# Two kinds of elementwise work of the recurrences go from VectorE to GpSimd

## The chip, the cores and the metric

The kernel runs on one core of a Trainium2 chip. The metric is the device time of one execution in microseconds (us), the median of several runs. The engines are named as in the profile: PE is TensorE (PEld its weight loads), DVE is VectorE, ACT is ScalarE, POOL is GpSimd, and SP is the engine from whose queue nearly all loads are issued.

## The reference

Two transformer blocks act on one sequence of 256 tokens with 1024 features, all in float32. The first block (a half feed-forward, a Hyena long convolution and differential attention side by side, another half feed-forward) is not touched by the change. The second block begins with a projection `u = h @ w_in`, whose columns feed several parts:

```python
u_rwkv = centred_token_shift(u[..., :RWKV_COLS], mu_prev, mu_next)
q, k_att, v_att, gl_rwkv, gl_attn = jnp.split(u[..., RWKV_COLS:], ATT_SPLITS, axis=-1)
y_rwkv = rwkv7_bidir(u_rwkv, ...)          # 8 heads of 64, one scan forward, one backward
y_attn = banded_gqa_attention(q, k_att, v_att, sink)
merged = sigmoid(gl_rwkv) * (y_rwkv @ w_proj_rwkv) + sigmoid(gl_attn) * (y_attn @ w_proj_attn)
x = x + merged @ w_out
x = x + expert_choice_moe(rms_norm(x, g), w_router, w_gate, w_up, w_down)   # 16 experts
return rms_norm(x, g_final)
```

One step of the scan, for each head, with a 64x64 state `S`:

```python
s_kk = jnp.einsum('bhij,bhj->bhi', S, kk_t)
S = S * w_t - s_kk[..., None] * (a_t * kk_t) + v_t[..., None] * k_t
y_t = jnp.einsum('bhij,bhj->bhi', S, r_t)
```

The expert part reads 16 x 3 matrices of 1024x1024 float32, some 200 MB, which no other part of the program approaches.

## The kernel before, in words

**Matmuls in three passes.** Where full float32 precision is wanted at a fast rate, a number is split into a high part (a cast by ACT, line 139) and a low part (the number less its high part, a subtraction with two inputs in SBUF, line 140). `mm3` (lines 145 to 147) multiplies high by high, high by low and low by high into one PSUM bank. `weights` (line 125) loads a chunk of weights into `raw` from SP's queue (line 130) and splits it in pieces of 128x512, into `whi` and `wlo`; for all weights DVE makes the low part. In the second block's pool there are two buffers each of `raw`, `whi` and `wlo`: a new load waits until the low part of the chunk two before has been made, and a new cast until PE is through with that chunk.

**The recurrences.** Instead of a scan over tokens, `lane` (line 1280) computes one direction of one pair of heads in four chunks of 64 tokens, with matmuls of 64x64. First it makes the decay products on PE (line 1296) and their exponentials on ACT, `W` and `Wv`; from these it makes four factors of 128x256: `t0`, `t1` (the factors of the rank-one updates and of the keys, lines 1307 to 1312) and the two halves of `kr` (line 1313: decay times normalised key, line 1314: decay times receptance). All on DVE. Matmuls of `kr` with `t0` and `t1` follow (line 1383, called from `mm_heads`), their masking on DVE (line 1323), then the inverse of a triangular matrix: a chain of 14 small DVE operations (lines 1426, 1427) and several products. Then four dependent steps of state and output, each a ping-pong between PE and DVE or ACT. `rwkv_out` normalises and gates the result; its last product, on DVE, is line 1489, after the matmul of the gates in line 1488.

There are eight such recurrences and four attention jobs. `lanes` (line 1225) keeps four of them active in four slots and takes one step of each in turn.

**The filling.** Between their steps it takes steps of the rest of the projection (`fill`): 22 chunks of 1024x128 weights for q, k, v and the gates, each 24 matmuls of 128x256, in two steps of 12. These `gemm_steps` are called with `whole=True`; no other call is. After the recurrences the outputs are split (`yh`, `yl`, line 140), projected with w_proj_rwkv and w_proj_attn, and so on. The loads of w_proj_attn, w_out and of all expert weights go to a ring of 41 buffers of 512 KB, whose memory is that of the recurrences' tiles.

**What sets the order.** The program's framework schedules each engine's queue itself from the order of the calls, the priorities and its own model of costs. A changed engine or cost therefore changes the order on all engines, also of instructions that the diff does not name.

Of the kernel before, what the change touches and what calls it, by code (L numbers as in the profile page):

```python
# [16 lines left out]
ALU = mybir.AluOpType  # L17
# [51 lines left out]
class Net:  # L69
# [52 lines left out]
        self.wp = self.pool(f"wp{n_raw}{n_split}", 1, side="left", es=self.wes)  # L122


    def weights(self, src, ring=False):

        nc = self.nc
        kt, cols = src.shape[1:]
        raw = self.raw_tile() if ring else self.wp.tile([128, kt, cols], F32, name="raw", tag="raw", bufs=self.n_raw)
        nc.sync.dma_start(out=raw, in_=src)  # L130
        hi = self.wp.tile([128, kt, cols], F32R, name="whi", tag="whi", bufs=self.n_split)
        lo = self.wp.tile([128, kt, cols], F32R, name="wlo", tag="wlo", bufs=self.n_split)
        n = max(1, min(kt, CUT // cols))
        for k in range(0, kt, n):
            self.split(raw[:, k:k + n], hi[:, k:k + n], lo[:, k:k + n])
        return hi, lo

    def split(self, src, hi, lo, eng=None):
# [14 lines left out]
    def gemm_steps(self, src, x, n, consume, c0=0, c1=None, steps=1, ring=False, whole=False):  # L153


        i = 0
        for c in range(c0, src.shape[0] if c1 is None else c1):
            hi, lo = self.weights(src[c], ring)
            kt, w = src.shape[2:]
            for m in range(w // 128):  # L160
                ps = self.mm([128, n])
                s = slice(m * 128, m * 128 + 128)
                for k in range(kt):
                    with self.tc.high_priority() if whole and k % (kt // steps) else ExitStack():
                        self.mm3(ps, (hi[:, k, s], lo[:, k, s]), (x[0][:, k, :], x[1][:, k, :]), k == 0, k == kt - 1)
                    if k < kt - 1 and (k + 1) % (kt // steps) == 0:
                        yield
                consume(i, ps)
                i += 1
                yield  # L170
# [290 lines left out]
    def first_ffn(self):  # L461
# [21 lines left out]
        with ExitStack() as es2:  # L483
# [13 lines left out]
            def weights(n):  # L497
# [3 lines left out]
                for i in range(2):  # L501
                    self.split(w[i][0][:, s], w[i][1][:, s], w[i][2][:, s])

            weights(0)
            diag = []
            for i in range(4):
# [16 lines left out]
            for f in range(KT + 1):  # L523
                if f < KT:
                    if f + 1 < KT:
                        raws.append(self.ada_load(f + 1, tmp))
                        if f % 2:
                            weights(f // 2 + 1)
                    row = self.ada_rows_of(raws[f], tmp)
                    ps = self.aux([128, 2 * T])  # L530
                    self.turned(ps, x, f, diag)
                if f:
                    products(f - 1, (0, 1))
                if f < KT:
                    a = self.ada_columns(f, row)
                    for i in range(2):
                        t = self.wk.tile([128, T], F32, name="nt", tag="nt", bufs=3)
                        nc.scalar.activation(out=t, in_=ps[:, cut[i]], func=AF.Identity, scale=a[:, i:i + 1],
                                             bias=self.mods[:, f, i:i + 1])
                        self.split(t, h[0][:, f, cut[i]], h[1][:, f, cut[i]])  # L540
                if f:
                    products(f - 1, (2, 3))
# [737 lines left out]
    def lane(self, L, p, d, ur):  # L1280

        nc = self.nc
# [3 lines left out]
        W, kr, Wv, t0, t1 = (L[x] for x in ("W", "kr", "Wv", "t0", "t1"))  # L1286
# [19 lines left out]
        a, kk = self.ar[:, d, p, :], self.kkn[:, p, :]  # L1306
# [3 lines left out]
        yield  # L1310
        nc.vector.tensor_tensor(out=t0, in0=t0, in1=Wv, op=ALU.mult)
        nc.vector.tensor_tensor(out=t1, in0=t1, in1=Wv, op=ALU.mult)
        nc.vector.tensor_tensor(out=kr[:, 0, :], in0=W[:, 1, :], in1=kk, op=ALU.mult)
        nc.vector.tensor_tensor(out=kr[:, 1, :], in0=W[:, 0, :], in1=ur[:, p, :], op=ALU.mult)
        yield

        for src, strict, incl in ((bb, ab, hb), (kh, ak, hk)):
# [659 lines left out]
```

## Time and profile before

| | |
|---|---|
| median of 3 runs | 1811.67 us (1810.1 to 1814.51) |
| the profiled execution itself | 1813.05 us |
| its span, first to last instruction | 1811.3 us |
| busy PE / DVE / ACT / POOL | 1687.9 / 1009.7 / 706.9 / 19.9 us |
| granted TensorE clock, mean | 0.925 |
| read from HBM | 394.59 MB, 218 GB/s over the span |

The profile is of one execution. Busy times are sums over instructions; matmuls overlap each other, so that a busy PE can still hold short stalls. A granted clock of 1.00 is TensorE's higher level, 2.4 GHz. The recurrences lie between about 1080 and 1275 us; up to there and a little beyond PE is nearly always busy, and from about 1290 us to the end DMA is.

### The profile page before, as it was taken

The page shows a single profiled execution, that of the slowest core. Times are in us where ns is not written, and L with a number is a line of the kernel's source. Part 1 is how long each engine was busy: PE and PEld are TensorE (multiplying, and loading weights), DVE is VectorE, ACT ScalarE, POOL GpSimd, SP SyncE. Part 2 cuts the span into 40 slices and gives each one's busy share as a digit, 9 for nine tenths or more (in the row PEclk, how much of TensorE's full clock was granted, in tenths as well). Part 3 has the DMA queues.
Part 4 walks back from the last instruction along what each step waited for, and adds up shares of the span by engine and source line. Part 5 has one row for each costly group of instructions (what it writes and reads, how often), then busy time and mean ns, then how long its engine had stood idle before and what let it go on. Part 6 is the DMA issues. An engine that isn't in the chain of part 4 may idle for free.

```text
span 1811.3 us, 33886 instructions
## 1 busy us (share of the span) xinstructions
PE 1687.9 (93%) x13847; PEld 1275.4 (70%) x13847; DVE 1009.7 (56%) x2502; ACT 706.9 (39%) x1515; POOL 19.9 (1%) x41
## 2 busy tenths in 40 slices
PE   8999999999999999999999999999999878787776
PEld 5788787788998889999999798888874222222222
DVE  3888776768987776676665768877740000000001
ACT  3532223657545568456444653456640000000001
POOL 0000000000000000000000000000010000000000
PEclk9999999999999999999999899999999676767678
DMA  8666673423432214546543331112799999999997
GB/s 330 217 219 231 220 260 112 133 82 121 155 108 94 91 70 140 187 148 248 187 163 117 115 123 61 49 61 76 298 400 400 409 408 409 409 408 409 408 409 303
DMA packets 97768, 397.85 MB, mean 220 GB/s; under 512 B 11227, under 2 KB 13708, under 8 KB 84044
## 3 DMA queue, kind: packets, MB, share of 16 engines
q1 hardware_dynamic: 91728, 386.97, 56.9%
q10 hardware_dynamic: 3724, 4.77, 0.8%
q0 software_dynamic: 2160, 3.94, 0.8%
q8 instruction: 109, 1.79, 0.4%
q14 instruction: 47, 0.39, 0.1%
HBM read 394.59 MB, written 1.05 MB: 218 GB/s over the span
## 4 chain that ended last, share of the span: by engine, by line
PE 68%; DMA 19%; DVE 8%; ACT 3%; issue 1%; DVEq 0%; ACTq 0%; SPq 0%
PE mm L145 13%; PE mm L147 12%; PE mm L146 12%; DMA raw<-exp_w_down 7%; DMA raw<-exp_w_gate 7%; PE mm L1572 4%; PE a L1383 4%; PE at L145 4%; PE at L146 4%; PE at L147 4%; PE a L1740 3%; DMA araw<-w_adat 2%; DMA raw<-exp_w_up 2%; DVE wlo L140 2%; DVE ajunk L310 2%
## 5 line engine op out<-in xcount | busy, mean ns | idle before, releaser
L139 ACT CAST whi<-raw 128x512 fp32r<-128x512 f32 x542 | 309.4, 618 | 260.6 <-PE mm L146 133.1
L140 DVE TENSOR_TENSOR wlo<-raw,whi 128x512 fp32r<-128x512 f32 x542 | 356.5, 686 | 97.8 <-ACT whi L139 93.5
L145 PE MATMUL mm<-hh,whi 128*128 128x256 f32 (+1 forms) x784 | 245.8, 315 | 0.5 <-DVE kl L140 0.5
L147 PE MATMUL mm<-hh,wlo 128*128 128x256 f32 (+1 forms) x784 | 244.9, 314 | 0.5 <-DVE wlo L140 0.2
L146 PE MATMUL mm<-hl,whi 128*128 128x256 f32 (+1 forms) x784 | 244.0, 312 | 0.0
L1707 DVE TENSOR_SCALAR scat<-iota,col 128x256 f32<-128x256 f32 x16 | 6.5, 412 | 275.0 <-PE a L1740 275.0
L145 PEld LDWEIGHTS mm<-hh,whi 128*128 128x128 f32 x784 | 147.2, 188 | 13.2 <-issue 3.5
L146 PEld LDWEIGHTS mm<-hl,whi 128*128 128x128 f32 x784 | 147.3, 188 | 9.9 <-issue 0.8
L147 PEld LDWEIGHTS mm<-hh,wlo 128*128 128x128 f32 x784 | 146.9, 188 | 10.0 <-DVE wlo L140 1.1
L1572 PE MATMUL mm<-raw,ehid 128*32 128x256 f32 x960 | 100.1, 513 | 40.6 <-DMA raw<-exp_w_down 40.2
L1744 ACT COPY ys<-mm 128x256 f32<-128x256 f32 (+1 forms) x20 | 7.2, 362 | 303.4 <-PE mm L1572 293.2
L310 DVE SCALAR_TENSOR_TENSOR ajunk<-araw,scr 128x512 bf16<-128x512 f32 x160 | 110.2, 689 | 27.6 <-DMA araw<-w_adat 25.5
L1572 PE MATMUL mm<-raw,xg 128*32 128x256 f32 x1024 | 103.1, 489 | 20.4 <-DMA raw<-exp_w_gate 20.4
L145 PE MATMUL at<-hh,whi 128*128 128x512 f32 (+1 forms) x352 | 118.7, 337 | 0.0
L147 PE MATMUL at<-hh,wlo 128*128 128x512 f32 (+1 forms) x352 | 118.4, 336 | 0.0
L146 PE MATMUL at<-hl,whi 128*128 128x512 f32 (+1 forms) x352 | 118.1, 336 | 0.0
L145 PE MATMUL mm<-whi,hidh 128*128 128x512 f32 x264 | 105.5, 400 | 1.1 <-ACT hidh L139 0.6
L147 PE MATMUL mm<-whi,hidl 128*128 128x512 f32 x264 | 104.8, 398 | 0.5 <-DVE hidl L140 0.4
L146 PE MATMUL mm<-wlo,hidh 128*128 128x512 f32 x264 | 104.8, 397 | 0.0
L1572 PEld LDWEIGHTS mm<-raw,ehid 128*32 128x32 f32 x960 | 23.7, 123 | 113.7 <-DMA raw<-exp_w_down 95.5
L1572 PE MATMUL a<-raw,xg 128*32 128x256 f32 x1024 | 83.9, 482 | 8.8 <-DMA raw<-exp_w_up 8.8
L145 PE MATMUL mm<-h2h,whi 128*128 128x256 f32 x296 | 89.7, 304 | 0.0
(630 smaller groups left out, 3391.9 us busy)
## 6 DMA issues: line engine op xcount, KB each, us to landing
raw<-exp_w_gate SPq DMA_DIRECT2D x128, 512.0 KB, 10.2
raw<-exp_w_up SPq DMA_DIRECT2D x128, 512.0 KB, 10.2
raw<-exp_w_down SPq DMA_DIRECT2D x120, 512.0 KB, 10.2
raw<-w_ff_in SPq DMA_DIRECT2D x42, 1024.0 KB, 4.8
raw<-w_in SPq DMA_DIRECT2D x32, 1024.0 KB, 4.7
araw<-w_adat SPq DMA_DIRECT2D x56, 512.0 KB, 4.7
raw<-w_ff_out SPq DMA_DIRECT2D x20, 1024.0 KB, 4.9
raw<-w_fill SPq DMA_DIRECT2D x22, 512.0 KB, 3.5
```

Of the source, the lines that this page charges most:

```text
L139: self.high = self.nc.scalar.copy(out=hi, in_=src)
L140: self.low = (eng or self.nc.vector).tensor_tensor(out=lo, in0=src, in1=hi.bitcast(F32), op=ALU.subtract)
L145: nc.tensor.matmul(out=ps, lhsT=w[0], rhs=x[0], start=first, stop=False)
L146: nc.tensor.matmul(out=ps, lhsT=w[0], rhs=x[1], start=False, stop=False)
L147: nc.tensor.matmul(out=ps, lhsT=w[1], rhs=x[0], start=False, stop=last)
L310: nc.vector.scalar_tensor_tensor(out=junk, in0=raw[:, s], scalar=1.0, in1=self.scr[v][:, s], op0=ALU.mult, op1=ALU.mult, accum_out=part[:, ...
L1383: self.nc.tensor.matmul(out=ps[r], lhsT=w[r], rhs=x[r], start=start, stop=stop)
L1572: nc.tensor.matmul(out=ps[q], lhsT=x(k), rhs=raw[:, j, :], start=(k == 0), stop=(k == KT - 1))
L1707: nc.vector.tensor_scalar(out=sc, in0=self.iota[:, 0:T], scalar1=col[:, 0, e:e + 1], scalar2=col[:, 1, e:e + 1], op0=ALU.is_equal, op1=ALU ...
L1740: nc.tensor.matmul(out=acc(tt, j), lhsT=sc[q, tt * 128:tt * 128 + 128], rhs=ys[q], start=False, stop=False)
L1744: nc.scalar.copy(out=ys, in_=ps)
```

## The change

Two edits. In `gemm_steps`, where `whole` is set, that is for the 22 chunks of the filling alone, the low parts of the weights are made by POOL instead of DVE. In `lane`, the two products that make `kr` are made by POOL.

```diff
-    def weights(self, src, ring=False):
+    def weights(self, src, ring=False, low=None):
...
-            self.split(raw[:, k:k + n], hi[:, k:k + n], lo[:, k:k + n])
+            self.split(raw[:, k:k + n], hi[:, k:k + n], lo[:, k:k + n], low)
...
-            hi, lo = self.weights(src[c], ring)
+            hi, lo = self.weights(src[c], ring, self.nc.gpsimd if whole else None)
...
-        nc.vector.tensor_tensor(out=kr[:, 0, :], in0=W[:, 1, :], in1=kk, op=ALU.mult)
-        nc.vector.tensor_tensor(out=kr[:, 1, :], in0=W[:, 0, :], in1=ur[:, p, :], op=ALU.mult)
+        nc.gpsimd.tensor_tensor(out=kr[:, 0, :], in0=W[:, 1, :], in1=kk, op=ALU.mult)
+        nc.gpsimd.tensor_tensor(out=kr[:, 1, :], in0=W[:, 0, :], in1=ur[:, p, :], op=ALU.mult)
```

`split` is not changed; its fourth argument is the engine of the low part, DVE if there is none.

The queues then look as follows. POOL at the start of the recurrences, before: a load, and copies for the inverse (`ip`), one set for each slot.

```order
L821 DMA rope<-rope 128x1024
L1403 COPY ip_10947<-r_10201 128x4x32
L1403 COPY ip_10965<-r_10201 128x4x32
L1403 COPY ip_10983<-r_10201 128x4x32
L1403 COPY ip_11001<-r_10201 128x4x32
```

POOL at the same place now (`wlo` are low parts of the filling, three numbers of `krs` three slots):

```order
L1403 COPY ip_10983<-r_10201 128x4x32
L1403 COPY ip_11001<-r_10201 128x4x32
L140 TENSOR_TENSOR wlo<-raw,whi 128x512
L1313 TENSOR_TENSOR krs_10949<-Ws_10948,kkn 128x256
L1314 TENSOR_TENSOR krs_10949<-Ws_10948,ur 128x256
L1313 TENSOR_TENSOR krs_10967<-Ws_10966,kkn 128x256
L1314 TENSOR_TENSOR krs_10967<-Ws_10966,ur 128x256
L1313 TENSOR_TENSOR krs_10985<-Ws_10984,kkn 128x256
L1314 TENSOR_TENSOR krs_10985<-Ws_10984,ur 128x256
L140 TENSOR_TENSOR wlo<-raw,whi 128x512 x4
```

Four low parts, of the first two chunks, stand before the products of the first three slots, and the next chunks' behind them. The queue goes on with low parts, products of the later recurrences and copies until the last low part, and then come the four loads of lines 1070 and 1073 that before stood right behind the last copy.

PE at the first use of the products, before (`mm<-h2` are fills, of which the last three of a step of 12 are shown):

```order
L145 MATMUL mm<-h2h_10176,whi 128x256
L146 MATMUL mm<-h2l_10184,whi 128x256
L147 MATMUL mm<-h2h_10176,wlo 128x256
L1383 MATMUL a_11033<-krs_10949,t0s_10951 64x128 x8
L1383 MATMUL a_11045<-krs_10949,t1s_10952 64x128 x8
L1383 MATMUL a_11134<-krs_10967,t0s_10969 64x128
L1388 MATMUL a_11056<-ident,t0s_10951 64x64 x6
```

PE at the same place now:

```order
L145 MATMUL mm<-h2h_10180,whi 128x256
L146 MATMUL mm<-h2l_10188,whi 128x256
L147 MATMUL mm<-h2h_10180,wlo 128x256
L1296 MATMUL a_11211<-rc,sg 128x2x128 x2
L1383 MATMUL a_11033<-krs_10949,t0s_10951 64x128 x8
L1383 MATMUL a_11045<-krs_10949,t1s_10952 64x128 x8
L1383 MATMUL a_11134<-krs_10967,t0s_10969 64x128 x2
L1388 MATMUL a_11056<-ident,t0s_10951 64x64 x6
```

A step of 12 fills that stood between the third decay product (line 1296) and the first use of `kr` now stands behind it. Over the whole stage the fills come later: 96 of the 528 stand behind the last recurrence's last matmul, where there were 58, and between the first decay product and the last fill there are 43 separate groups of fills instead of 50.

DVE at the end of the stage, before (`yh`, `yl` are low parts of the outputs, `wlo` here those of w_proj_rwkv):

```order
L1485 TENSOR_TENSOR t1s_11006<-ur,a_13913 128x256
L140 TENSOR_TENSOR yl_14084<-q_10197,yl_14080 128x256
L1486 TENSOR_TENSOR t0s_11005<-t0s_11005,t1s_11006 128x256
L140 TENSOR_TENSOR yl_14085<-q_10197,yl_14081 128x256
L1489 TENSOR_TENSOR ur<-t0s_11005,a_13918 128x256
L140 TENSOR_TENSOR wlo<-raw,whi 128x512 x4
L140 TENSOR_TENSOR yh_14077<-ur,yh_14073 128x256
L1087 TENSOR_TENSOR gates<-mm,gates 128x256 x2
```

DVE at the same place now:

```order
L1489 TENSOR_TENSOR ur<-t0s_11005,a_13918 128x256
L140 TENSOR_TENSOR wlo<-raw,whi 128x512
L140 TENSOR_TENSOR yl_14082<-q_10197,yl_14078 128x256
L140 TENSOR_TENSOR yh_14074<-ur,yh_14070 128x256
L140 TENSOR_TENSOR yh_14075<-ur,yh_14071 128x256
L140 TENSOR_TENSOR yh_14076<-ur,yh_14072 128x256
L140 TENSOR_TENSOR yh_14077<-ur,yh_14073 128x256
L140 TENSOR_TENSOR yl_14083<-q_10197,yl_14079 128x256
L140 TENSOR_TENSOR yl_14084<-q_10197,yl_14080 128x256
L140 TENSOR_TENSOR yl_14085<-q_10197,yl_14081 128x256
L140 TENSOR_TENSOR wlo<-raw,whi 128x512 x3
```

The last recurrence's output (line 1489) now stands before all splits and before three of the four low parts of w_proj_rwkv. On PE the gates' matmul (line 1488), which line 1489 reads, stands before the last 24 fills, where it stood behind the last fill and four projection matmuls. On SP's queue one load of w_proj_attn now stands between the second and the third load of w_proj_rwkv; all four stood behind the fourth.

## Rows read from the trace of the kernel before

**Rows 1.** Page, chain of waits; table of stretches: engine busy (x instructions), clock, DMA.

```profile
PE 68%; DMA 19%; DVE 8%; ACT 3%; issue 1%; DVEq 0%; ACTq 0%; SPq 0%
...
1090.00:1120.00 30.00, 29.42 (x600) 26.24 (x597) 25.09 (x106) 11.45 (x31) 0.30 (x1) 1.00 0.23 73
...
1240.00:1270.00 30.00, 30.00 (x290) 24.05 (x286) 22.18 (x66) 20.59 (x49) 0.00 (x0) 1.00 0.22 71
```

**Rows 2.** Waits of PE's weight loads, 1080 to 1275: us, times, longest; first and last.

```profile
PEld a L1383 <- issue: 2.6, 9, 0.4
...
PEld a L1472 <- PE mm L146: 0.2, 1, 0.2
```

**Rows 3.** DVE's groups, 1080 to 1290: busy us, mean ns, idle before.

```profile
L140 DVE TENSOR_TENSOR wlo<-raw,whi 128x512 fp32r<-128x512 f32 x51 | 34.1, 686 | 9.5 <-ACT whi L139 9.3
...
L1314 DVE TENSOR_TENSOR krs<-Ws,ur 128x256 f32<-128x256 f32 x8 | 3.4, 420 | 0.0
```

**Rows 4.** Timeline of PE near the end of the filling: start, length, instruction.

```profile
1272.52 0.28 PE L146 MATMUL mm<-h2l,whi 128*128 128x256 f32 x1
1272.64 0.28 PE L147 MATMUL mm<-h2h,wlo 128*128 128x256 f32 x1
1272.90 0.68 PE L1472 MATMUL a<-ident,yall 64*64 64x64 f32 x16
1273.51 0.39 PE L145 MATMUL mm<-h2h,whi 128*128 128x256 f32 x1
1273.73 0.28 PE L146 MATMUL mm<-h2l,whi 128*128 128x256 f32 x1
```

**Rows 5.** Timeline of ACT, DVE and PE at the first recurrence's start.

```profile
1079.57 0.60 ACT L1298 ACTIVATE Ws<-a 128x512 f32<-128x512 f32 x1
...
1081.61 0.42 DVE L1313 TENSOR_TENSOR krs<-Ws,kkn 128x256 f32<-128x256 f32 x1
...
1082.68 0.42 DVE L1314 TENSOR_TENSOR krs<-Ws,ur 128x256 f32<-128x256 f32 x1
...
1083.66 1.09 PE L1383 MATMUL a<-krs,t0s 64*64 64x128 f32 x16
```

**Rows 6.** Timeline of POOL and DVE in the routing stage.

```profile
1336.86 6.00 POOL L140 TENSOR_TENSOR hm<-hf,hm 128x256 fp32r<-128x256 f32 x8 [4.34 <-ACT hm L139]
...
1338.48 0.42 DVE L1641 MAX8 top<-at 16x8 f32<-16x256 f32 x1
...
1340.35 0.55 DVE L1647 TENSOR_TENSOR sel<-top,slotmask 16x128 f32<-16x128 f32 x1
...
1344.29 0.26 DVE L1647 TENSOR_TENSOR sel<-top,slotmask 16x128 f32<-16x128 f32 x1
```

**Rows 7.** Timeline of PE, DVE and SP's queue after the filling.

```profile
1274.93 0.28 PE L147 MATMUL mm<-h2h,wlo 128*128 128x256 f32 x1
...
1277.64 2.49 DVE L140 TENSOR_TENSOR wlo<-raw,whi 128x512 fp32r<-128x512 f32 x4
...
1278.38 0.38 PE L147 MATMUL mm<-yh,wlo 128*128 128x256 f32 x1 [1.24 <-DVE wlo L140]
...
1280.05 0.42 DVE L140 TENSOR_TENSOR yh<-ur,yh 128x256 fp32r<-128x256 f32 x1
...
1280.58 2.00 SPq L130 DMA_DIRECT2D raw<-w_proj_attn  x4
...
1281.74 0.28 DVE L1098 TENSOR_TENSOR wr<-wr,pv 128x128 f32<-128x128 f32 x1
```

**Rows 8.** Table of stretches, the first in which loads run without pause.

```profile
1290.00:1340.00 50.00, 47.71 (x366) 43.50 (x365) 31.39 (x75) 27.46 (x71) 3.66 (x5) 0.96 1.03 409
```

**Rows 9.** Waits of SP's queue, 1284 us to the end.

```profile
SPq L1564 <- DMA raw<-exp_w_gate: 112.2, 124, 2.3
...
SPq L1564 <- PE mm L1572: 12.8, 19, 4.6
```

**Rows 10.** Timeline of POOL: the first and last of the routing's loads.

```profile
1235.37 0.54 POOL L1070 DMA_DIRECT2D iota<-iota  x1 [87.10 <-PE a L1383]
...
1236.95 0.95 POOL L1073 DMA_DIRECT2D wr<-w_router  x1
```

## The prediction, before the change was run

> **What bounds the kernel now.** I read the chain of waits first: 68% of it is TensorE (PE) and 19% DMA, only 8% VectorE (DVE) [rows 1]. So the question for each part of the program is which of the two it belongs to. The change touches the recurrences and the projection that fills them, from about 1080 to 1275 us. The table by stretches shows there that PE is busy 29.4 of 30.0 us in one stretch and 30.0 of 30.0 in another, at a granted clock of 1.00, while DVE is busy 25.1 and 22.2 [rows 1]. Busy PE can hide stalls, so the list of what PE's weight loads waited for comes next: 25 rows from 1080 to 1275 us, 13.6 us in sum, the longest single wait 0.4 us [rows 2]. Those of the 25 that end on DVE sum to 4.0 us, and PE's own three rows add 0.7. The recurrences are bound by the number of matmuls in PE's queue. DVE, which the change relieves, works 137.4 of 180 us in the six stretches of 30 us of which two are shown, and has a quarter of its time free.
>
> Behind them the program is bound by DMA: from 1290 us on the queues move 409 GB/s [rows 8], and what SP's queue waits for are its own earlier transfers, 112.2 us for the gate weights alone, against 12.8 us for PE [rows 9]. What counts at the end is therefore when this stream begins. It begins at 1280.58 us with the first load of w_proj_attn, which goes to a buffer of the expert ring [rows 7].
>
> **Part by part.**
>
> *Low parts to POOL.* 22 chunks of two halves are 44 subtractions of 128x512. On DVE one takes 686 ns [rows 3], so 30.2 us leave DVE. POOL has no such row; the nearest is the same subtraction at 128x256, eight in 6.00 us, 0.75 us each [rows 6]. A 128x512 lies between 0.75 (all of it fixed cost) and 1.50 us (no fixed cost); I take 1.50, as these eight ran end to end: 66 us of POOL. Cost on the path: nothing, if the low parts come in time. A chunk is 24 fill matmuls of 0.12 us spread over some 9 us (195 us for 22), and two buffers stand ahead; a half that comes 0.8 us later is covered by the chunk in front of it. In the dense end of the filling, four chunks now follow each other with 2.9 us of PE work each, and POOL needs 3.0 for a chunk; the two chunks already split when it begins cover that. If that cover were gone, four times 0.1 plus one latency of 1.5 us, some 2 us, would show.
>
> *Products to POOL.* 16 of 128x256 at 420 ns [rows 3], 6.7 us off DVE, 12 us onto POOL. Here the path is near. The decay tile is ready for POOL at about 1080.2 us (exponential at 1079.57, 0.60 long), DVE makes the two products at 1081.61 and 1082.68, and PE starts on them at 1083.66, 0.56 us after the second ends [rows 5]. Now 12 fill matmuls less stand ahead of that start, so PE arrives 1.5 us sooner, at 1082.1. POOL's pair takes 1.5 us: ready at 1081.7 if it runs alone, at 1083.2 if each of the two loses its own length to DVE, which works without a pause there. So PE waits 0 to 1.1 us; DVE's factor, needed at the same place, comes at 1082.1 as before. I take 0.7. Later starts have more room, since POOL is then between chunks.
>
> *DVE relieved.* 36.9 us less work there. DVE is not the bound, so this itself is worth 0 to 4.7 us, the PE waits above that end on it.
>
> *DVE and POOL side by side.* No row of the recurrences shows POOL beside DVE for long; the routing stage does. While POOL ran its eight subtractions, an operation of DVE with two inputs in SBUF (sel) took 0.55 us, and 0.26 once POOL had stopped; MAX8, with one input, took 0.42 [rows 6]. So a POOL operation can hold such an instruction up by 0.29 us or, at twice the length, 0.58. Summed over all POOL work that is 44 x 0.58 + 16 x 0.29 = 30 us, less than the 36.9 that leave: DVE is no more loaded than now. On the path: PE has 16 waits on DVE in its two lists; POOL is busy 78 of 195 us, 40%, so 6 of them meet it and grow by 0.29 to 0.58, 1.9 to 3.7 us; and the DVE queue in front of them is 27% shorter (36.9 of 137.4), which takes 1.3 of their 4.7 away. Net 0.6 to 2.4; I take 1.0. The outer bounds are below nothing, -4.7, and +12, which is rival C.
>
> The Trainium skill (SBUF — State Buffer, Who interferes with whom) says that a DVE instruction with two SBUF inputs and a GpSimd instruction that reads SBUF share one read interface, and that whichever starts first keeps it until it ends. The sel rows agree in direction, and MAX8 with its one input agrees too. By that rule the longest delay is a whole POOL operation, 1.50 us instead of 0.58; rival C is what this would make of it. The Trainium skill (GPSIMD Engine Reference, Elementwise — side-by-side cycle accounting) gives 2.6 cycles an element for two inputs; an estimate from that page puts a 128x512 at 1.3 us, and POOL's work at 69 instead of 78 us, which would change no term.
>
> *The order on PE.* The scheduler groups the fills anew: 50 separate groups between the first decay product and the last fill before, 43 now. Entering a group costs 0.22 instead of 0.12 us from its first matmul to the next, and leaving it 0.26 instead of 0.12 [rows 4]: 0.24 us a group. Seven fewer: -1.7 us. Behind the last recurrence 96 fills remain instead of 58, and the output product of the gates (L1488, 0.6 us) now stands before the last fill, four projection matmuls (0.5 us) behind it: +0.1.
>
> *The hand-over to the stream.* Before, the last fill starts at 1274.93 us. DVE does the split of the outputs, then four low parts at 1277.64, then the last split at 1280.05, on which SP's load at 1280.58 waits; PE itself stands until 1278.38 [rows 7]. The stream starts 5.6 us after the last fill. Now L1488 runs 24 fills, 2.9 us, before the last one, so the output it completes comes early: after it DVE has one product (0.33 from start to start), one low part (0.6) and eight splits (0.33 each): they end 2.9 - 0.6 - 0.33 - 0.6 - 2.7, that is 1.3 us after the last fill. Then three low parts of 0.6 release the last two buffers of w_proj_rwkv, and the stream follows 3.2 us after the last fill: -2.4 us. SP also has one w_proj_attn load ahead of the last two w_proj_rwkv; 0.5 MB at 409 GB/s is 1.3 us, which may come on top. Bounds 0 (the ring fills before the routing is done, and waits) and -3.7.
>
> *POOL's own queue.* Four small loads for the routing stand behind the filling's last low part now, where they ran at 1235 to 1238 us [rows 10]. That part belongs to the last chunk, whose buffer comes free two chunks earlier, 7.1 us before the last fill; a cast of 0.6 and two halves of 1.5 later is 3.5 us before it, near 1271.4; 2.6 us of issue and 3 to land give 1277, ahead of their first reader at 1281.74 [rows 7]. Nothing.
>
> Sum: 0.7 + 1.0 - 1.7 + 0.1 - 2.4 = -2.3 us. The profiled execution took 1813.05 us itself (span 1811.3), so 1810.75; it lies 1.38 above the median of the runs, and on their scale that is **1809.4 us**.
>
> **Rivals.**
>
> A. *Nothing arrives.* The regrouped order saves on one side what it stalls on the other, and the earlier stream only fills the ring sooner: 19 waits of SP on PE, 12.8 us [rows 9], show that the ring does run full once. Against it: the rest of the stream waits on DMA alone, and PE's projection starts sooner as well. 1811.7 us.
>
> B. *DVE's share counts in full.* The 4.7 us of PE waits on DVE go, no product is late, and the stream gains its full 3.7: -4.7 - 1.7 + 0.1 - 3.7 = -10.0, less 1 for what is certain to remain: 1802.7 us. For it: each of these waits is short and right behind a DVE instruction. Against it: two-input work of DVE stays, and POOL now meets it.
>
> C. *Slower: POOL holds the inverses.* Each of the eight recurrences has one chain of 14 small two-input operations on DVE (L1426, L1427) that nothing else can overtake, at the end of which PE waits. If in each one POOL operation starts first and keeps DVE out for its whole 1.50 us, and PE has nothing else in its queue at that point, that is 8 x 1.5 = 12 us; with the other terms -3.3 it is +8.7, 1820.4 us. It passes the 0.3% if six of the eight reach PE in full. For it: PE's queue is fixed in order, and sel was held. Against it: sel lost 0.29 of the 0.75 a POOL operation lasts, and PE mostly has another recurrence or a fill in front.
>
> **How the numbers follow.** Forecast 47% (from 1806 to 1813), A 17%, B 18%, C 13%, something else 5%. A difference below 0.3%, 5.4 us, can't be told from none here. Faster by more than that: B and the lower edge of the forecast, 24%. Slower: C and half of the rest, 17%. No difference: 59%. The range for 8 in 10 reaches nearly to B and C: 1803 to 1818; the forecast's own is 1806 to 1813.
>
> **What would show it.** In the profile after: POOL busy near 80 us between 1065 and 1275, DVE some 37 us less; PE's weight loads still waiting about 14 us in that stretch; the first w_proj_attn load at about 1278 instead of 1280.6, all later loads shifted alike; 128x512 on POOL between 1.2 and 1.5 us. The forecast is wrong if PE's waits on DVE, or on POOL's low parts, exceed some 8 us (C), if POOL takes over 2 us for a half, or if the stream starts before 1276 (B).

## The result, and the profile after

The changed kernel takes **1835.29 us** (median of 4 runs, 1833.12 to 1838.39) against 1813.09 (1810.1 to 1816.13): a ratio of 1.0119, 95% interval 1.0096 to 1.0141. It is slower by some 22 us, and outside the range of 1803 to 1818. The profiled execution took 1835.68 us, its span 1833.5, 22.2 longer than before.

Busy times of the whole span, from the page of the changed kernel:

```profile
PE 1693.5 (92%) x13847; PEld 1275.5 (70%) x13847; DVE 1009.8 (55%) x2442; ACT 706.9 (39%) x1515; POOL 90.0 (5%) x101
```

POOL has 70 us more, as the change says. DVE lost 36.9 us of work and is busy for as long as before (1009.7). So its other instructions became longer. The groups of POOL and DVE in the stage of the recurrences (columns as in [rows 3]) show which:

```profile
L140 POOL TENSOR_TENSOR wlo<-raw,whi 128x512 fp32r<-128x512 f32 x44 | 57.1, 1316 | 678.1 <-ACT whi L139 678.1
L1314 POOL TENSOR_TENSOR krs<-Ws,ur 128x256 f32<-128x256 f32 x8 | 6.7, 842 | 0.0
...
L1357 DVE COPY t0s<-a 128x64 f32<-128x64 f32 x32 | 6.7, 220 | 8.3 <-PE a L1383 8.3
L1412 DVE TENSOR_REDUCE cps<-Wvs 128x32 f32<-128x256 f32 x8 | 4.9, 614 | 0.0
L1426 DVE TENSOR_TENSOR subs<-kt,nts 128x16 f32<-128x16 f32 x8 | 3.4, 430 | 0.1
L1301 DVE COPY sms<-Ws 128x4 f32<-128x4 f32 x8 | 2.9, 362 | 1.5 <-ACT Ws L1298 1.5
```

The same two small groups of the kernel before:

```profile
L1426 DVE TENSOR_TENSOR subs<-kt,nts 128x16 f32<-128x16 f32 x8 | 1.4, 171 | 0.1
L1301 DVE COPY sms<-Ws 128x4 f32<-128x4 f32 x8 | 1.3, 164 | 0.0
```

The copy out of PSUM (221 ns before) and the reduction with one input (612 before) kept their length; the small subtractions with two inputs in SBUF and the copy from SBUF to SBUF more than doubled in the mean. The mean hides what happens to a single one. The timeline of an inverse, while POOL makes two low parts:

```profile
1097.82 2.49 POOL L140 TENSOR_TENSOR wlo<-raw,whi 128x512 fp32r<-128x512 f32 x2 [13.60 <-ACT whi L139]
1098.27 0.85 DVE L1427 TENSOR_TENSOR nts<-nts,subs 128x20 f32<-128x20 f32 x1
...
1099.16 1.18 DVE L1426 TENSOR_TENSOR subs<-kt,nts 128x16 f32<-128x16 f32 x1
...
1100.38 0.17 DVE L1427 TENSOR_TENSOR nts<-nts,subs 128x16 f32<-128x16 f32 x1
...
1101.35 0.68 PE L1383 MATMUL a<-Wvs,Ws 64*64 64x64 f32 x16 [1.26 <-DVE Wvs L1439]
```

An operation of 0.17 us takes 0.85, the next one 1.18, which is nearly a whole low part (2.49 for two); with POOL done, they are back at 0.17. TensorE stands for 1.26 us behind them. The first recurrence shows the same (it answers to [rows 5]):

```profile
1077.23 0.90 POOL L1314 TENSOR_TENSOR krs<-Ws,ur 128x256 f32<-128x256 f32 x1
...
1078.89 0.94 DVE L1309 TENSOR_TENSOR t0s<-ar,kkn 128x256 f32<-128x256 f32 x1
...
1080.62 0.68 DVE L1301 COPY sms<-Ws 128x4 f32<-128x4 f32 x1
1081.21 0.41 DVE L1311 TENSOR_TENSOR t0s<-t0s,Wvs 128x256 f32<-128x256 f32 x1
...
1081.77 1.97 PE L1383 MATMUL a<-krs,t0s 64*64 64x128 f32 x16 [4.57 <-DVE t0s L1311]
```

POOL's product for this matmul is done at 1078.1. What comes late is DVE's factor of line 1311: it ends 10.0 us after the start of the first decay product (1071.58). Before, where the first decay product starts at 1076.68, it was 5.8:

```profile
1082.01 0.42 DVE L1311 TENSOR_TENSOR t0s<-t0s,Wvs 128x256 f32<-128x256 f32 x1
```

The list of waits of TensorE's weight loads, 1080 to 1275 us, has 30.2 us in 28 rows ([rows 2]: 13.6); 13.6 of them end on DVE, where it was 4.0. Its longest:

```profile
PEld a L1383 <- POOL krs L1314: 4.9, 1, 4.9
PEld a L1383 <- DVE ak L1354: 4.5, 5, 2.4
PEld a L1383 <- DVE Wvs L1366: 2.7, 2, 2.2
```

(The first of them is the wait just shown; the list names POOL, whose product had long been done.) Where TensorE stands for long, its granted clock falls too:

```profile
1078.00:1084.00 6.00, 2.23 (x22) 2.26 (x24) 6.00 (x9) 1.19 (x4) 6.00 (x7) 0.79 0.18 74
1114.00:1120.00 6.00, 3.66 (x72) 3.42 (x70) 5.82 (x18) 2.15 (x5) 2.49 (x2) 0.91 0.12 34
```

**The account.** Take the stage from the start of the first decay product to that of the last matmul of fills or gates: 1076.68 to 1276.77 before, 200.1 us; 1071.58 to 1294.73 now, 223.2. That is +23.1. TensorE's busy time and granted clock over the stage, before and then now (columns as in [rows 1]), divide it:

```profile
1076.00:1277.00 201.00, 199.94 (x3286) 174.63 (x3284) 155.56 (x560) 105.41 (x257) 3.73 (x8) 1.00 0.19 62
```

```profile
1071.00:1295.00 224.00, 206.56 (x3283) 179.72 (x3281) 155.71 (x498) 102.44 (x250) 73.39 (x71) 0.97 0.17 57
```

TensorE stands for 17.4 us where it stood for 1.1, and is busy for 6.6 us longer with the same matmuls, at a mean granted clock of 0.97 instead of 1.00. So some 16 us of the 23.1 are standing, and the rest are matmuls at the clock that fell while it stood.

The execution had come to the stage 5.1 us earlier, with nothing changed up to there; that is scatter between executions, since in e7 below, which is the kernel before up to that point, the stage begins at 1071.84. Then the stream starts late (this answers to [rows 7]):

```profile
1288.54 2.81 SPq L130 DMA_DIRECT2D raw<-w_proj_rwkv  x2
1291.45 0.38 SPq L130 DMA_DIRECT2D raw<-w_proj_attn  x1
1297.49 1.67 SPq L130 DMA_DIRECT2D raw<-w_proj_rwkv  x2
1299.21 1.38 SPq L130 DMA_DIRECT2D raw<-w_proj_attn  x3
1300.63 7.94 SPq L130 DMA_DIRECT2D raw<-w_out  x8
```

The first w_out load is 5.9 us behind the stage's end in both (1282.62 and 1300.63). From it to the end of the span are 528.7 us before and 532.9 now, +4.2. Sum: 23.1 - 5.1 + 4.2 = 22.2.

### The profile page after: what moved, and what is told of

It is laid out like the page before. It is cut to its first block, busy times and chain, and to the rows that moved or that the text cites. A ratio compares the mean times of both kernels' runs of the same rounds, so it can differ in the third digit from the quotient of the medians.

```text
span 1833.5 us, 33907 instructions
## 1 busy us (share of the span) xinstructions
PE 1693.5 (92%) x13847; PEld 1275.5 (70%) x13847; DVE 1009.8 (55%) x2442; ACT 706.9 (39%) x1515; POOL 90.0 (5%) x101
## 4 chain that ended last, share of the span: by engine, by line
PE 64%; DMA 22%; DVE 10%; ACT 3%; issue 2%; POOL 0%; ACTq 0%; DVEq 0%; SPq 0%; POOLq 0%
PE mm L145 13%; PE mm L147 12%; PE mm L146 12%; DMA raw<-exp_w_down 7%; DMA raw<-exp_w_gate 7%; DMA raw<-exp_w_up 4%; PE at L145 4%; PE at L146 3%; PE at L147 3%; PE a L1383 3%; PE mm L1572 2%; DMA araw<-w_adat 2%; PE a L1740 2%; DVE ajunk L310 2%; DVE wlo L140 1%
## 5 line engine op out<-in xcount | busy, mean ns | idle before, releaser
L140 DVE TENSOR_TENSOR wlo<-raw,whi 128x512 fp32r<-128x512 f32 x498 | 327.2, 686 | 85.8 <-ACT whi L139 82.7
```

The costliest lines, as they stand in the source:

```text
L140: self.low = (eng or self.nc.vector).tensor_tensor(out=lo, in0=src, in1=hi.bitcast(F32), op=ALU.subtract)
```

## The experiments

Theory H: each POOL operation keeps DVE out of SBUF until it ends. Theory O: the new order of the queues costs the time. Theory L: POOL's products come late. From e5 on H and O are left, and from e7 there is a theory K besides: TensorE's clock comes back late in the routing, and that costs time. "Stage" is the time defined above, "rest" that from the first w_out load to the end, both of the profiled execution; the ratio is that of all runs to before's on the same chip.

| kernel | stage | rest | ratio (95%) |
|---|---|---|---|
| before | 200.1 | 528.7 | |
| changed | 223.2 | 532.9 | 1.0119 (1.0096 to 1.0141) |
| e1 low parts only | 216.1 | 532.8 | 1.0120 (1.0101 to 1.0139) |
| e2 products only | 204.8 | 528.4 | 1.0029 (1.0018 to 1.0041) |
| e3 shadow | 216.5 | 533.3 | 1.0106 (1.0089 to 1.0123) |
| e4 quarters | 212.8 | 533.1 | 1.0078 (1.0064 to 1.0092) |
| e5 narrow | 206.1 | 529.2 | 1.0048 (1.0030 to 1.0067) |
| e6 write only | 202.1 | 533.9 | 1.0029 (1.0015 to 1.0043) |
| e7 before, idle matmuls | 200.0 | 527.9 | 1.0005 (0.9993 to 1.0016) |
| e8 changed, idle matmuls | 222.3 | 529.7 | 1.0135 (1.0120 to 1.0151) |
| e9 narrow, idle matmuls | 206.0 | 528.1 | 1.0029 (1.0020 to 1.0039) |
| e10 write only, idle matmuls | 202.1 | 528.7 | 1.0019 (1.0006 to 1.0032) |
| e11 relief alone | 201.4 | 529.7 | 1.0011 (1.0000 to 1.0022) |
| e12 late chunks | 201.3 | 534.9 | 1.0027 (1.0015 to 1.0039) |

Four kernels ran twice with nothing changed in the stage (before and e7, changed and e8, e5 and e9, e6 and e10): it agrees within 0.1 us in three pairs, 0.9 in the fourth. It is the finer measure here. The rest is a coarser one, since the profiled execution is not the median one: those of e1, e2, e5, e7 and e8 took 2 to 5 us less than the median of their runs, that of e12 3 us more.

**e1, e2: one part alone.**

```diff
# e1, against the changed kernel
-        nc.gpsimd.tensor_tensor(out=kr[:, 0, :], in0=W[:, 1, :], in1=kk, op=ALU.mult)
-        nc.gpsimd.tensor_tensor(out=kr[:, 1, :], in0=W[:, 0, :], in1=ur[:, p, :], op=ALU.mult)
+        nc.vector.tensor_tensor(out=kr[:, 0, :], in0=W[:, 1, :], in1=kk, op=ALU.mult)
+        nc.vector.tensor_tensor(out=kr[:, 1, :], in0=W[:, 0, :], in1=ur[:, p, :], op=ALU.mult)
# e2, against the changed kernel
-            hi, lo = self.weights(src[c], ring, self.nc.gpsimd if whole else None)
+            hi, lo = self.weights(src[c], ring)
```

> Low parts on POOL, the two products back on DVE. Its order on TensorE differs from the changed kernel's in 43 of 7,856 rows. Theory H (a POOL operation keeps DVE out of SBUF until it ends, and TensorE waits for DVE's chains): 57.1 of POOL's 70.2 us of such work stay, so four fifths of the 22 us: 1827 to 1834. Theory O (the new order of the queues costs the time): 1835, as the changed kernel. Theory L (POOL's products come late, TensorE waits for them, 4.9 us at the first recurrence): 1829 or less, with no long stall at the first recurrence.

> The two products on POOL, the low parts back on DVE. Its order on TensorE is that of the kernel before but for some 90 of 7,853 rows. Theory H: 13.1 of 70.2 us of POOL's work stay: 1814 to 1820. Theory O: 1813, as before. Theory L: the late first product stays, with its 4.7 us and some for the seven others: 1818 to 1822.

The times are 1832.2 and 1816.4 us, as H said, with stages of +16.0 and +4.7. In e1 the stall at the first recurrence falls from 4.57 to 1.0 us, as L said, but the time stays; and in e2, with the products on POOL, TensorE waits only 0.2 us for the first recurrence's factors, and its longest wait, 3.2 us, is for a low part of DVE's. So L fails. O stands with e1, and misses e2, whose order is nearly that of before, by some 5 us. The changed kernel's stage is 7 us longer than e1's and its ratio the same; the runs don't resolve this.

**e3: POOL works for nobody.**

```diff
# against before; the passing on of `shadow`, a part of the gates' tile, is left out
             self.split(raw[:, k:k + n], hi[:, k:k + n], lo[:, k:k + n])
+            if shadow is not None: nc.gpsimd.tensor_tensor(out=shadow, in0=hi[:, k:k + n].bitcast(F32),
+                                                           in1=hi[:, k:k + n].bitcast(F32), op=ALU.subtract)
```

> The kernel before, with DVE still making all low parts, and POOL besides making 42 subtractions of 128x512 of each high part with itself into a part of the gates' tile that is written in full later: nobody waits for POOL, and TensorE's and DVE's queues are in the order of the kernel before. Theory H: 42 x 1.25 = 52 us in which DVE is kept out, and it is not relieved of anything: as slow as the changed kernel or slower, 1830 to 1855, with the small DVE operations of the inverse at 0.3 to 0.5 us in the mean. Theories O and L: no change, 1811 to 1815.

The time is 1831.4 us, the stage +16.4: this is the loss with TensorE's and DVE's queues in the order of before and with no one waiting for POOL. O and L can't make it; this run decides for H. Its timeline:

```profile
1099.05 2.16 POOL L135 TENSOR_TENSOR gates<-whi 128x512 f32<-128x512 f32 x2 [15.12 <-ACT whi L139]
1099.51 0.62 DVE L1426 TENSOR_TENSOR subs<-kt,nts 128x24 f32<-128x24 f32 x1
1100.39 0.86 DVE L1427 TENSOR_TENSOR nts<-nts,subs 128x24 f32<-128x24 f32 x1
1101.51 0.17 DVE L1426 TENSOR_TENSOR subs<-kt,nts 128x20 f32<-128x20 f32 x1
```

**e4: smaller pieces.**

```diff
# against the changed kernel
-            self.split(raw[:, k:k + n], hi[:, k:k + n], lo[:, k:k + n], low)
+            if low is None: self.split(raw[:, k:k + n], hi[:, k:k + n], lo[:, k:k + n])
+            else: nc.scalar.copy(out=hi[:, k:k + n], in_=raw[:, k:k + n]), [low.tensor_tensor(out=lo[:, j], in0=raw[:, j], ...) for j in range(k, k + n)]
```

> The changed kernel, but POOL makes each low part in four pieces of 128x128 instead of one of 128x512; TensorE's and DVE's queues are in the same order as in the changed kernel, and POOL's work is longer in sum by the fixed cost of 132 more operations. Theory H: a DVE operation is kept out for one piece, about 0.37 us, not 1.25, and gets its turn between two: 1816 to 1827. Theory O: 1835. Theory L: the low parts come later than now: 1835 to 1840.

The time is 1826.8 us, at the edge of what H gave, with a stage of +12.7 instead of +23.1. A piece takes 0.48 us, not the 0.37 expected, so POOL works 78.7 us on low parts instead of 57.1; and 26 of the 112 operations of the inverses exceed 0.3 us instead of 11, the longest 0.71 instead of 1.23. Shorter holds, but more of them.

**e5, e9: POOL's operations cut down; e7, e8, e10: TensorE kept busy in the routing.** (WARM are the numbers of idle matmuls that the routing puts on TensorE between its steps, line 1839.)

```diff
# e5, against the changed kernel (kr likewise: 32 of 256 columns; the tile of an earlier chunk as `lo` is left out)
-            self.split(raw[:, k:k + n], hi[:, k:k + n], lo[:, k:k + n], low)
+            w = slice(0, 8 if low and c > 1 else cols)
+            nc.scalar.copy(out=hi[:, k:k + n], in_=raw[:, k:k + n])
+            (low or nc.vector).tensor_tensor(out=lo[:, k:k + n, w], in0=raw[:, k:k + n, w], ...)
# e7 to e10, against before, changed, e5, e6
-WARM = 4, 8, 4
+WARM = 6, 15, 9
```

> The changed kernel in its order (TensorE's queue differs in 8 rows of 7,856, all in the projection behind the filling), with POOL's operations cut down: from the third chunk on it makes only the first 8 of each 128 columns of a low part (the rest keeps the values of an earlier chunk), and 32 of the 256 columns of each product (the rest is zero, set once), so its output is not the reference's. DVE is relieved as in the changed kernel and hardly held. Theory H: the loss goes, and what DVE's relief and the new order are worth by themselves is left: 1803 to 1812. Theory O: the order stays, and so the loss: 1830 to 1835.

e5 took 1819.3 us, above what H gave and below what O gave. The stage is 17.1 us shorter than the changed kernel's and still +6.0; 3.5 us of that is one stall of TensorE at the first recurrence, where POOL had four whole low parts and the setting of four tiles to zero in front. DVE's factors stand behind an operation that this kernel's POOL held:

```profile
1072.50 1.28 POOL L135 TENSOR_TENSOR wlo<-raw,whi 128x512 fp32r<-128x512 f32 x1 [0.33 <-ACT whi L134]
...
1073.23 2.56 DVE L1307 TENSOR_SCALAR t1s<-ar,pv,omk 128x256 f32<-128x256 f32 x1
...
1073.72 1.93 POOL L1237 MEMSET krs<- 128x512 f32 x4
```

The scaling of line 1307 (a TENSOR_SCALAR, which reads one tile) took 2.56 us instead of 0.41, until just behind the end of the four MEMSETs, which read nothing; in the changed kernel, which has none, it took 0.69. e11 takes these low parts and MEMSETs away.

> The kernel before, with more idle matmuls on TensorE in the routing (9 instead of 4, 15 instead of 8, 6 instead of 4 at the three places), everything else in the same order. In the profiles of before and of the products alone TensorE is back at a granted clock of 1.00 some 6 us after the reciprocal of line 1602, in those of the other kernels only after 18 us, and the first expert matmul comes 4.6 us later. Theory K (this later return costs up to 5 us of the time, and hits some executions of every kernel): with TensorE kept busy all executions are of the good kind, 1805 to 1809, 0.1 to 0.3% faster than before. Without K (the ring of buffers hides it): 1810.

> The changed kernel with the same idle matmuls. Theory H with K: of the 22 us some 4.5 are the routing's clock, which the idle matmuls take away: 1828 to 1832; the 18.6 us of the later stream stay. Without K: 1835.

> The narrow kernel (POOL's operations cut down, the changed kernel's order, output not the reference's) with the same idle matmuls. Theory H with K: the 9 us that it was slower than before came from the routing's clock in most of its executions, and DVE's relief and the order are worth nothing or little: 1803 to 1810. Theory O: the new order itself costs some 9 us: 1817 to 1821.

The times are 1811.9 (e7), 1834.3 (e8) and 1815.8 us (e9). In the profiles K has a place: the rest falls from 532.9 to 529.7 (changed), 533.9 to 528.7 (write only, e6 and e10). In the times it hardly has: e8 shows no gain, and e7, whose kernel has no such delay in its profile, none either; e10 and e9 gain some 2 and 3.5 us, but the intervals of each pair overlap. e7 and e8 came out as forecast without K, and e9 fits neither of its forecasts. K explains little of the 22 us.

**e6, e10: POOL writes and doesn't read.**

```diff
# e6, against e3
-nc.gpsimd.tensor_tensor(out=shadow, in0=hi[:, k:k + n]..., in1=hi[:, k:k + n]..., op=ALU.subtract)
+nc.gpsimd.tensor_tensor(out=shadow[:, :, 0:1], in0=hi[:, k:k + n, 0:1]..., ...), nc.gpsimd.memset(shadow, 0.0), nc.gpsimd.memset(shadow, 0.0)
```

> As the shadow kernel, with the order of the kernel before on TensorE and DVE, but POOL's 42 subtractions of 128x512 are each replaced by one of 128x4, which waits for the high part as they did, and two fills of 128x512 with zero, which read nothing: about 1.2 us of POOL as before. Theory H in its plain form (any POOL operation keeps DVE out): 1825 to 1832, as the shadow kernel. H by reads (an operation of DVE with two inputs in SBUF is kept out only by a POOL operation that reads SBUF; at most its copies and scalings meet one that writes): 1811 to 1818, with the small operations of the inverse at 0.17 us throughout.

> The kernel whose POOL operations write only, with the same idle matmuls. H by reads with K: the 5 us that it was slower were the routing's clock, so the time of the kernel before with idle matmuls, within 2 us: 1805 to 1811. If POOL's work costs 5 us even without reading: 5 us more than that kernel.

The times are 1817.4 (e6, as H by reads said) and 1815.4 us (e10); the stage is +2.0 where the shadow kernel had +16.4, with POOL busy 62.8 us in it instead of 56.7. The inverse beside it keeps its pace:

```profile
1097.54 1.11 POOL L135 MEMSET gates<- 128x512 f32 x2
1097.73 0.17 DVE L1426 TENSOR_TENSOR subs<-kt,nts 128x24 f32<-128x24 f32 x1
1098.15 0.17 DVE L1427 TENSOR_TENSOR nts<-nts,subs 128x24 f32<-128x24 f32 x1
```

None of the 112 exceeds 0.19 us. So what holds the two-input operations is POOL's reading, as H by reads said. The Trainium skill (SBUF — State Buffer, Who interferes with whom) states this split: two SBUF inputs on DVE against a GpSimd instruction that reads, not one that only writes; and copies in its two-port modes among the held, reductions not. These traces agree, for the two-input operations in e3 and e6, and in the changed kernel in the copy of 164 to 362 ns and in the reduction of 612 and 614.

Writing alone was not quite free, though. e10 missed its forecast (1805 to 1811); by the ratios it is some 2.5 us slower than e7, which has the same idle matmuls, with intervals that overlap, and both e6 and e10 have 2 us more in the stage. DVE's scalings did grow in e6. The mean of this group was 349 ns before; the longest, beside a MEMSET, took 698:

```profile
L1536 DVE TENSOR_SCALAR s1s<-s1s,sms 128x256 f32<-128x256 f32 x8 | 3.5, 477 | 0.0
```

Over all scalings of the stage this is some 3 us of DVE's time. That it makes the 2 us of the stage is not shown.

**e11, e12: the relief alone, and the last chunks alone.**

```diff
# e11, against e5: products and the first two chunks on DVE
+            (low if low and c > 1 else nc.vector).tensor_tensor(...)
# e12, against e1
+            hi, lo = self.weights(src[c], ring, self.nc.gpsimd if whole and c > 15 else None)
```

> DVE's relief without the hold: the products and the low parts of the first two chunks stay on DVE, and of the other 40 low parts POOL makes only 8 of each 128 columns (the rest keeps an earlier chunk's values, so the output is not the reference's). 27 us of work leave DVE, and POOL's 40 operations take 0.28 us each. TensorE's order differs in some 60 rows from that of the kernel with the low parts alone on POOL, whose stage from the first decay product to the last matmul of filling or gates took 216.1 us (before: 200.1). Theory H: nearly all of the 16 us go, the stage takes 198 to 202 us, the time is 1808 to 1813: the relief itself is worth 0 to 2 us. Theory O (the new order costs some 6 us, as the narrow kernel's 206.1 us suggest): 204 to 207 us, 1815 to 1819.

> Low parts on POOL for the last 6 of the 22 chunks alone, 12 operations, all behind the last inverse; the products on DVE. In the changed kernel the stretch behind its last inverse lost under 1 us against before, though 9 chunks' low parts fell into it. Theory H, where it counts what DVE has to do: 1810 to 1813, no slower than before. H as a price for each operation alike (16 us for 44): 4 us more than before, 1814 to 1816.

e11 took 1812.7 us, with a stage of 201.4, both as H said. This is e1 almost without the hold, in nearly its order, so that 14.7 of e1's 16.0 us come from the hold; and 27 us less work on DVE, together with the new order, gain nothing. Table of stretches, the stage in e1 and then in e11 (columns as in [rows 1]):

```profile
1071.00:1287.00 216.00, 202.73 (x3275) 176.41 (x3274) 152.51 (x511) 101.36 (x247) 61.33 (x55) 0.98 0.18 58
```

```profile
1075.00:1277.00 202.00, 199.71 (x3281) 174.26 (x3280) 135.33 (x519) 103.25 (x252) 15.65 (x48) 1.00 0.19 62
```

TensorE is idle for 13.3 us in e1 (216.00 less 202.73), at a clock of 0.98, and for 2.3 in e11, at 1.00. DVE is busy 17 us less in e11, though it has four low parts more to make.

e12 took 1816.9 us, above both expectations, though the stage is only +1.2 for 15.3 us of POOL, as H counted: behind the inverses few operations of DVE meet it that TensorE waits for. In the profiled execution the loss lies in the rest, 534.9. The routing in before, then in e12:

```profile
1336.46:1342.46 6.00, 5.46 (x14) 2.08 (x15) 5.83 (x20) 3.03 (x10) 5.60 (x8) 0.50 1.03 411
1342.46:1348.46 6.00, 6.00 (x36) 4.17 (x35) 3.52 (x15) 2.78 (x7) 0.40 (x1) 0.95 1.02 408
1348.46:1354.46 6.00, 6.00 (x62) 4.47 (x62) 2.25 (x3) 2.07 (x3) 0.00 (x0) 1.00 0.97 362
```

```profile
1336.46:1342.46 6.00, 4.95 (x13) 1.93 (x14) 5.83 (x18) 2.73 (x9) 5.65 (x8) 0.50 1.03 411
1342.46:1348.46 6.00, 6.00 (x17) 2.87 (x16) 3.17 (x14) 3.10 (x9) 0.26 (x1) 0.50 1.02 408
1348.46:1354.46 6.00, 6.00 (x27) 5.55 (x26) 0.61 (x2) 0.18 (x1) 0.00 (x0) 0.50 0.68 270
```

At the same times, TensorE has 0.50 of its clock (1.2 GHz) for 12 us longer in e12 and does less than half as many matmuls (17 and 27 instead of 36 and 62), and the stream is at 270 instead of 362 GB/s. Before that it had stood in both kernels (1.43 and 1.15 us at 1337.0), waiting for the routing's small steps. Why it gets its clock back sooner in some kernels than in others stays open, and so does how much of e12's 5 us this explains: its profiled execution lies above the median, and in e8 and e10 the idle matmuls changed the profile more than the time.

No version with POOL at work came out ahead of the kernel before, and the relief gains nothing even where it is nearly free of the hold.

## Why the prediction was wrong

- **What bounds the stage**: right for the kernel before, where TensorE stands for 1.1 us of the stage. With 27 of the 36.9 us of relief and hardly a hold, e11 gains nothing.
- **DVE and POOL side by side**: this step failed. It said "a POOL operation can hold such an instruction up by 0.29 us or, at twice the length, 0.58", counted 6 of 16 waits, and took 1.0. The 0.29 was what was left of a POOL operation when sel came to it [rows 6]: the operation ran from 1340.04 to 1340.76, sel from 1340.35. It was not the price of a whole one. The runs show the whole length: up to 1.23 us for an operation of 0.17, and each low part of a pair holds the next operation of the chain again. The term is 14.7 us for the low parts (e1 less e11), 16.4 with the order of before (e3), and with the products most of 23.1. The prediction's own sign of being wrong came with it: 13.6 us of waits on DVE, above the 8.
- **Rival C** had the mechanism and a cost of 12 us, one POOL operation for each inverse. It was given 13%, in part because of the same 0.29. In the trace it is not the inverses alone: of TensorE's waits, those on lines 1354 and 1366 lie in the state steps (7.2 us), and the longest at the first recurrence. The rule of the Trainium skill that I set against the row was right to the full length, and so was the estimate from its page GPSIMD Engine Reference (Elementwise — side-by-side cycle accounting), 1.3 us for a low part, of which the rate of 2.6 cycles an element alone is 1.11 (1.316 measured in the mean; I took 1.50).
- **Products**: 0.7 us forecast at the first recurrence, 4.57 measured. TensorE was free at 1077.2 and POOL's pair done at 1078.1, so that POOL's part of the wait is within the forecast; DVE's own factor, held several times on its way, came at 1081.6. (The forecast had that factor "at 1082.1 as before"; in the trace of before it ends at 1082.43.)
- **Low parts in time**: right; no wait of TensorE on POOL's low parts is among the 28 rows, nor later in the stage.
- **Order on PE**: -1.7 forecast, not found. With the hold nearly gone, the stage is 1.3 us longer (e11), not shorter. Of the fills, 96 stand behind the last recurrence there too, so that its state steps have fewer between them; that this is the 1.3 us was not tested.
- **Hand-over**: -2.4 forecast; 5.9 us from the stage's end to the first w_out load, as before. The prediction's mark, the first load of w_proj_attn, starts at 1291.45, before the stage's end, but the other three wait until 1299.21. The early order didn't help, since the first loads of w_proj_rwkv wait for raw buffers that POOL's last low parts free: one of these ends at 1288.52, and the first load starts at 1288.54, 6.2 us before the last fill, where it was 10.4. The third load then waits for DVE's low part of the first, until 1297.46.
- **POOL's routing loads**: right, at no cost; they end at 1293.5, their first reader starts at 1299.56.
- **Not foreseen**: the rest behind the stream, +4.2 us in this execution. The profile puts it on the clock in the routing; the time of e8 does not bear that out, so it stays open.
- **The chances**: "slower" was given 17%, but C and half of the rest make 15.5%.

## What to carry to other kernels

In these runs work moved from DVE to POOL wasn't free for DVE when both read SBUF: price every meeting at the full length of the POOL operation, and look first at chains of tiny two-input operations, where 0.17 us becomes 1.2. One short overlap in a trace bounds that price from below only. Before moving work off an engine that doesn't bound the stage, ask what its free time is worth; a cut-down copy of the moved work, as e11, answers it in one run, and a shadow that nobody waits for, as e3, shows the cost by itself.

## What the runs showed of the hardware that was not expected

- A POOL operation that only writes (128x512 in 0.53 us, e6) left DVE's two-input operations of the inverse at 0.17 us; one that reads (1.28 us, e3) stretched them to up to 1.03.
- POOL operations that only write did hold DVE's scalings, which read one tile: 2.56 us instead of 0.41 across four MEMSETs in a row (e5), and up to 0.70 instead of 0.35 (e6).
- A POOL subtraction of 128x128 takes 0.48 us beside DVE, one of 128x512 1.32: four small ones cost 1.5 times the large one.
- In the routing, TensorE's clock stood at 0.50 for 6 us in one kernel and for 18 in another (before and e12), with the same work and nearly the same times. In the profiles of the kernels with the long stretch the rest is 4 to 6 us longer; their times show less of it.
